# Another order of the gate/up products in two Strassen-Winograd FFNs

## The chip, the cores and the metric

The kernel runs on one core of a Trainium2 chip, in one launch. The metric is device time in microseconds, the median of several runs; lower is better.

## The reference, cut to what matters

One layer of a hybrid decoder on 1024 prompt tokens and 8 decode tokens (1032 rows of width 1024): a SwiGLU feed-forward network (FFN) at half weight, then attention beside a state-space mixer, cross-attention, a second FFN, and a final norm. The change lies in the two FFNs, which have weights of their own and the same code:

```python
def swiglu(x, w_gate, w_up, w_down):
    return (jax.nn.silu(x @ w_gate) * (x @ w_up)) @ w_down

x = x + (0.5 * swiglu(rms_norm(x, g_ffn1), w1_gate, w1_up, w1_down)).astype(x.dtype)
```

The width is 1024, the inner width 2816. Everything is float32.

## The kernel before, in words

**Layout and products.** Activations stand transposed, features on the partitions. The tokens are cut into two large groups of 388 (P0, P1) and a rest of 256 (R). Each float32 operand is split into a high and a low part (`put`, line 273, for activations; `split`, line 302, for weights): ScalarE rounds the high part, and VectorE or GpSimd subtracts it to get the low part, in turn for weights. `three` (line 315) makes one product of 128 x 128 from three matmuls: high by high, high by low, low by high.

**Seven products for eight.** The two large groups are multiplied by Winograd's form of Strassen's scheme, 2 x 2 blocks. The weights' blocks are A11, A12 (the two halves of the gate weights' contraction) and A21, A22 (the same of the up weights). `SUMS` (line 294) makes S1 = A21 + A22, S2 = S1 - A11, S3 = A11 - A21 and S4 = A12 - S2. On the activations' side stand B11, B21, B22 and the sums T1 to T4. The seven products are A11 by B11, S2 by T2, A12 by B21, S3 by T3, S1 by T1, S4 by B22 and A22 by T4. `ORDER` (line 322) gives their order in the program, the PSUM bank of each (0, 1, 2 for b1, b2, b3), and whether it begins a bank.

**A gate/up unit** (`gate_up`, line 356, 22 in each FFN) makes 128 inner columns. It loads the gate and the up weights by one DMA each (`raw_`, line 310), 512 KB each, into a ring of two buffers. For each name `mat` (line 365) forms a sum if one is needed and splits it; the split weights go through a ring of four buffers. The program calls for S1's split just ahead of S3's sum, because S3's sum takes S1's place in the buffer of sums, and multiplies S1 after S3. A product is four times `three`, 12 matmuls of 388 columns. For A11, A12, A22 and A21 the rest of the tokens is multiplied as well (`rest`, line 372), 12 matmuls of 256 columns each, in a bank of its own. `evac` (line 384) empties the banks: A11's product is copied from b1 to b2; after S2 the contents of b2 are kept as U2 by a ScalarE copy (line 389); after A12 b1 is gate group P0, through Silu (line 392); after S3 b2 is kept as U3 by a ScalarE copy (line 395); after S1 VectorE adds b3 and U3 to make u1, up group P1 (line 398); S4 goes on in b3, and b3 + U2 is gate group P1 (line 401), whose Silu (402) times u1 (403) is a hidden block; A22 goes on in b2 and gives the last hidden block (line 415). So S4's products need b3 read by the add of line 398, which needs U3.

The hidden blocks are made into the operands of the down stage: lines 408 and 411 and the `put`s of T2, B22 and T3 follow S4, line 421 and T4 follow A22.

**The down stage** (`down`, line 450) comes after every two units. It takes two blocks of the down weights, through the same rings, and the same seven products in an order of its own, 6 matmuls each for two output blocks at a time. Its evacuations are VectorE adds to the residual (lines 490 to 507) and ScalarE copies from one bank to another (line 488); a copy needs the bank emptied by the add of line 500 of the output blocks before. The last pair of units has another down stage (`down_last`, line 522).

**Queues.** The order in which the program calls is not the order of the queues: the kernel is built with `tile.TileContext(nc, schedule_with_timeline_sim=True)` (line 1833), a planner that simulates the engines and writes each engine's queue, taking the earliest call that it holds ready. Each engine then works through its queue in order, so an instruction that waits holds up those behind it. Loads are issued by SyncE.

Of the kernel before, what the change touches and what calls it, by code (L numbers as in the profile page):

```python
# [28 lines left out]
PA = 388  # L29
# [47 lines left out]
def tile_step(ctx, tc, a, o):  # L77
    nc = tc.nc
# [28 lines left out]
    def ring(tag, bufs, width):  # L107
        return lambda n=344: tp.tile([128, width], F32, name=tag, tag=tag, bufs=bufs)[:, :n]

    sq_, acc_, g1_, u1_ = ring("tu", 4, PA), ring("ts", 3, PA), ring("tg", 2, PA), ring("tv", 2, 344)  # L110
# [147 lines left out]
    def cols_of(w, c, n=128):  # L258
        return w.rearrange("(k p) n -> p k n", p=128)[:, :, c:c + n]
# [13 lines left out]
    def put(dst, src, eng):  # L273
        nc.scalar.copy(dst[0], src)
        eng.tensor_sub(dst[1], src, dst[0].bitcast(F32))
# [21 lines left out]
    def two(n):  # L297

        t = wt("fw", F32R)
        return t[:, :n], t[:, n:2 * n]  # L300

    def split(hl, src, like=lambda t: t):

        hi, lo = like(hl[0]), like(hl[1])
        st["turn"] = not st.get("turn")
        nc.scalar.copy(hi, src)  # L306
        (nc.vector if st["turn"] else nc.gpsimd).tensor_sub(lo, src, hi.bitcast(F32))  # L307
        return hl

    def raw_(src):  # L310
        t = wp.tile([128, 1040], F32, name="fraw", tag="wr", bufs=2)[:, :1024]
        st["load"] = nc.sync.dma_start(t if len(src.shape) == 2 else t.rearrange("p (k c) -> p k c", c=src.shape[2]), src).ins
        return t

    def three(ps, w, j, v, start, stop):

        js = slice(j * 128, (j + 1) * 128)
        for i, (l, m) in enumerate(((w[0], v[0]), (w[0], v[1]), (w[1], v[0]))):
            nc.tensor.matmul(ps, l[:, js], m, start=bool(start and not i), stop=bool(stop and i == 2), skip_group_check=True)  # L319


    ORDER = (("A11", 0, "B11", True), ("S2", 1, "T2", False), ("A12", 0, "B21", False), ("S3", 1, "T3", False),
             ("S1", 2, "T1", True), ("S4", 2, "B22", False), ("A22", 1, "T4", False), ("A21", None, None, False))

    def hid(name, dt=F32):
        return st["fh"].tile([128, PA], dt, name=name, tag="hP", bufs=14)

    def ffn(x, F, wg, wu, wd, fin, turn, mid=None, rest_in=None):
# [3 lines left out]
        def sums_of(m):  # L332
            if not m:
                return wt("fs", F32)
            if not held:
                held.append(rp.tile([128, T], F32, name="fs", tag="r"))
            return held[0]
# [8 lines left out]
        def bank_set():  # L346
            st["set"] = not st.get("set")
            return sets[st["set"]]

        def add_up(name, t, at):  # L350
            p, q, op = SUMS[name]
            t[name] = dst = at
            nc.vector.tensor_tensor(dst, t[p], t[q], op=op)  # L353
            return dst

        def gate_up(m):
            q = m % 2
            g_, u_ = raw_(cols_of(wg, m * 128)), raw_(cols_of(wu, m * 128))
            t = {"A11": g_[:, :512], "A12": g_[:, 512:], "A21": u_[:, :512], "A22": u_[:, 512:]}
            bk, rb = bank_set()  # L360
            b1, b2, b3 = bk
            sums = sums_of(m)
            e = {}

            def mat(name):
                if name == "S2":
                    add_up("S1", t, sums[:, :512])
                if name in SUMS and name not in t:
                    add_up(name, t, sums[:, :512] if name == "S3" else sums[:, 512:1024])
                return split(two(512), t[name])  # L370

            def rest(name, w):
                i = name in ("A21", "A22")
                first, last = name in ("A11", "A22"), name in ("A12", "A21")
                for j in range(4):
                    three(rb[:, int(i)], w, j, F["R"][j + (4 if name in ("A12", "A22") else 0)], first and j == 0, last and j == 3)

            def rest_end():
                gr, hr = u1_(NR), u1_(NR)
                nc.scalar.activation(gr, rb[:, 0], AF.Silu)  # L380
                nc.vector.scalar_tensor_tensor(hr, rb[:, 1], 0.5, gr, op0=OP.mult, op1=OP.mult)
                put(Hd["R"][q], hr, nc.vector)

            def evac(name):
                if name == "A11":
                    nc.scalar.copy(b2, b1)
                elif name == "S2":
                    e["U2"] = acc_(PA)
                    nc.scalar.copy(e["U2"], b2)
                elif name == "A12":  # L390
                    e["g0"] = g1_(PA)
                    nc.scalar.activation(e["g0"], b1, AF.Silu)
                elif name == "S3":
                    e["U3"] = acc_(PA)
                    nc.scalar.copy(e["U3"], b2)  # L395
                elif name == "S1":
                    e["u1"] = sq_(PA)
                    nc.vector.tensor_add(e["u1"], b3, e["U3"])  # L398
                elif name == "S4":
                    g1, u1 = g1_(PA), e["u1"]  # L400
                    nc.vector.tensor_add(g1, b3, e["U2"])
                    nc.scalar.activation(g1, g1, AF.Silu)
                    nc.vector.scalar_tensor_tensor(u1, u1, 0.5, g1, op0=OP.mult, op1=OP.mult)
                    if Hd["plain"]:
                        put(Hd["B22" if q else "B12"], u1, nc.vector)
                    elif q:
                        b12, t1 = Hd["b"]
                        nc.vector.tensor_sub(t1, u1, t1)
                        put(Hd["T2"], t1, nc.vector)
                        put(Hd["B22"], u1, nc.gpsimd)  # L410
                        nc.vector.tensor_sub(b12, u1, b12)
                        put(Hd["T3"], b12, nc.gpsimd)
                elif name == "A22":
                    u0, u1 = sq_(PA), e["u1"]
                    nc.vector.scalar_tensor_tensor(u0, b2, 0.5, e["g0"], op0=OP.mult, op1=OP.mult)
                    put(Hd["B21" if q else "B11"], u0, nc.vector)
                    if Hd["plain"]:
                        pass
                    elif q:
                        t2 = Hd["b"][1]  # L420
                        nc.vector.tensor_sub(u0, u0, t2)
                        put(Hd["T4"], u0, nc.gpsimd)
                    else:
                        nc.vector.tensor_sub(u0, u1, u0)
                        put(Hd["T1"], u0, nc.gpsimd)
                        Hd["b"] = (u1, u0)

            late = m == 0
            early = {}
            for name, b, f, first in ORDER:  # L430
                if late and name == "A21":
                    continue
                if name == "S3":
                    early["S1"] = mat("S1")
                w = early.pop(name, None) or mat(name)
                if f:
                    for j in range(4):
                        three(bk[b], w, j, F[f][j], first and j == 0, j == 3)
                if f:
                    evac(name)  # L440
                if name[0] == "A" and not late:
                    rest(name, w)
            if late:
                if rest_in:
                    rest_in(sets[not st["set"]][0][2])
                for name in ("A11", "A12", "A22", "A21"):
                    rest(name, mat(name))
            rest_end()
# [90 lines left out]
        for m in range(0, DFF // 128, 2):  # L539
            for nm in MATS if m < last else ("B11", "B12", "B21", "B22"):  # L540
                Hd[nm] = tuple(hid(nm + i, F32R) for i in "hl")
            Hd["R"] = [tuple(st["fh"].tile([128, NR], F32R, name="hR" + i, tag="hR", bufs=4) for i in "hl") for _ in range(2)]
            Hd["plain"] = m == last
            for i in range(2):
                with nullcontext():
                    gate_up(m + i)
                if mid:
                    mid(m + i)
            if m < last:
                with nullcontext():  # L550
                    down(m)
            else:
                turn()
                down_last(m)
# [1282 lines left out]
```

## Time and profile before

| | us |
|---|---|
| median of 3 runs | 2673.5 (2665.6 to 2675.37) |
| the profiled execution | 2677.61 |
| its span | 2675.8 |
| TensorE busy | 2517.3 |
| VectorE busy | 1797.9 |
| ScalarE busy | 1172.5 |
| GpSimd busy | 911.8 |

The profile shows one execution, with times from the start of its span. TensorE's busy time is that of its matmuls, which are pipelined, so that rows of it overlap; a matmul's real price in a full stream is the distance from one start to the next. The first FFN lies between about 100 and 810 us, the second between 1927 and 2640 us. On line 319 the operand's name tells the product: names with a digit at the end, such as T40h, are the factors of the gate/up units (T4, block 0, high part), names without it, such as T2h, those of the down stage; R0 to R7 are the rest of the tokens in gate/up units, hR in down stages.

### The profile page before, as it was taken

The numbers are of one execution on the slowest core, as the hardware profiler recorded it, in microseconds if no ns is written. First come the engines' busy times: TensorE is split into PE (matmuls) and PEld (weight loads), VectorE is DVE, ScalarE is ACT, GpSimd is POOL, SyncE is SP. The second block draws the span as 40 slices with busy tenths as digits, with TensorE's granted clock in tenths as the row PEclk, the third lists the DMA queues.
The fourth block names the chain that finished last, engine by engine and source line by source line (L and its number), as shares of the span: only waits on it lengthen the run. The fifth ranks groups of instructions, "written<-read, shape, count | busy, mean of one in ns | idle before, by whom it ended". The sixth has DMA issues, their size and how long they took to land.

```text
span 2675.8 us, 42135 instructions
## 1 busy us (share of the span) xinstructions
PE 2517.3 (94%) x15999; PEld 2391.8 (89%) x15999; DVE 1797.9 (67%) x3648; ACT 1172.5 (44%) x2413; POOL 911.8 (34%) x687
## 2 busy tenths in 40 slices
PE   6899999999999999999897899989889999999998
PEld 5899999999998899999686798879789999999997
DVE  7566666666667676778578867565686666666665
ACT  5433333333334455554477523232443333333345
POOL 5433333333325111115265664101643333333333
PEclk9999999999999999999898999999999999999999
DMA  5411211112113222227666634573111111111112
GB/s 171 136 49 57 62 60 57 57 57 64 57 48 105 75 69 78 87 74 236 199 196 221 211 94 134 170 219 116 34 48 48 48 48 49 55 48 51 53 48 80
DMA packets 273748, 252.13 MB, mean 94 GB/s; under 512 B 17392, under 2 KB 243880, under 8 KB 273536
## 3 DMA queue, kind: packets, MB, share of 16 engines
q1 hardware_dynamic: 271872, 249.34, 30.3%
q8 instruction: 126, 2.06, 0.3%
q14 instruction: 78, 0.64, 0.1%
q10 hardware_dynamic: 1672, 0.09, 0.0%
HBM read 204.25 MB, written 49.98 MB: 95 GB/s over the span
## 4 chain that ended last, share of the span: by engine, by line
PE 69%; DVE 14%; DMA 8%; issue 3%; ACT 3%; POOL 2%; SPq 0%; DVEq 0%; ACTq 0%; POOLq 0%
PE fb L319 44%; PE pqkv L255 5%; PE pxbc L255 4%; PE pcq L255 2%; PE pco L255 2%; DMA fraw<-in_w_up_dram 2%; PE pwa L255 2%; PE po L1061 1%; DVE fs L353 1%; PE ps L1035 1%; PE ptr L1055 1%; PE pzz L255 1%; DMA cqb<-cq_scr 1%; DVE ckv L1531 1%; DMA kb<-in_cache_win_k_dram 1%
## 5 line engine op out<-in xcount | busy, mean ns | idle before, releaser
L245 POOL TENSOR_TENSOR wl<-wr,wh 128x1024 fp32r<-128x1024 f32 (+4 forms) x79 | 165.5, 2095 | 569.9 <-ACT wh L241 542.4
L307 POOL TENSOR_TENSOR fw<-fraw,fw 128x512 fp32r<-128x512 f32 x131 | 174.7, 1333 | 467.4 <-ACT fw L306 387.8
L307 POOL TENSOR_TENSOR fw<-fs,fw 128x512 fp32r<-128x512 f32 x128 | 172.5, 1348 | 398.6 <-ACT fw L306 351.0
L306 ACT CAST fw<-fs 128x512 fp32r<-128x512 f32 x256 | 158.2, 618 | 272.6 <-PE fb L319 161.3
L306 ACT CAST fw<-fraw 128x512 fp32r<-128x512 f32 x262 | 162.2, 619 | 186.2 <-PE fb L319 182.2
L353 DVE TENSOR_TENSOR fs<-fraw 128x512 f32<-128x512 f32 (+1 forms) x168 | 103.4, 615 | 136.0 <-DMA fraw<-in_w_up_dram 67.3
L307 DVE TENSOR_TENSOR fw<-fraw,fw 128x512 fp32r<-128x512 f32 x131 | 102.2, 780 | 113.0 <-ACT fw L306 113.0
L307 DVE TENSOR_TENSOR fw<-fs,fw 128x512 fp32r<-128x512 f32 x128 | 96.2, 752 | 94.4 <-ACT fw L306 94.4
L319 PE MATMUL fb<-hRh,fw 128*128 128x256 f32 x640 | 137.3, 280 | 0.4
L241 ACT CAST wh<-wr 128x1024 fp32r<-128x1024 f32 (+1 forms) x80 | 76.8, 960 | 117.8 <-PE pwa L255 29.7
L319 PEld LDWEIGHTS fb<-hRh,fw 128*128 128x128 f32 x640 | 109.2, 188 | 3.6 <-DVE x L505 3.6
L255 PE MATMUL pxbc<-xh,wh 128*128 128x344 f32 x288 | 94.0, 326 | 2.0 <-DVE xr L872 2.0
L255 PE MATMUL pqkv<-xh,wh 128*128 128x344 f32 x288 | 93.8, 326 | 0.3 <-DVE x L535 0.3
L255 PE MATMUL pxbc<-xl,wh 128*128 128x344 f32 x288 | 93.5, 325 | 0.0
L255 PE MATMUL pqkv<-xh,wl 128*128 128x344 f32 x288 | 93.1, 323 | 0.0
L255 PE MATMUL pqkv<-xl,wh 128*128 128x344 f32 x288 | 92.9, 323 | 0.0
L255 PE MATMUL pxbc<-xh,wl 128*128 128x344 f32 x288 | 92.9, 323 | 0.0
L319 PE MATMUL fb<-hRl,fw 128*128 128x256 f32 x320 | 87.7, 278 | 0.0
L398 DVE TENSOR_TENSOR tu<-fb,ts 128x388 f32<-128x388 f32 x44 | 24.7, 562 | 90.2 <-ACT ts L395 90.2
L1042 ACT ACTIVATE pr<-pr,nm 128x128 f32<-128x128 f32 (+3 forms) x64 | 49.7, 777 | 55.3 <-DVE nm L1040 55.0
L319 PE MATMUL fb<-T2h,fw 128*128 128x388 f32 x160 | 54.2, 359 | 18.7 <-ACT fb L488 18.7
L1040 DVE CUSTOM_DVE_ANT_0 pr<-ps,U 128x128 f32<-128x128 f32 (+3 forms) x64 | 48.1, 751 | 27.2 <-PE ps L1035 16.9
(806 smaller groups left out, 9420.3 us busy)
## 6 DMA issues: line engine op xcount, KB each, us to landing
fraw<-in_w_gate_dram SPq DMA_DIRECT2D x44, 512.0 KB
fraw<-in_w_up_dram SPq DMA_DIRECT2D x44, 512.0 KB
fraw<-in_w_down_dram SPq DMA_DIRECT2D x44, 512.0 KB
wr<-in_w_in_dram SPq DMA_DIRECT2D x32, 512.0 KB
x_scr<-x SPq DMA_DIRECT2D x16, 516.0 KB
x<-x_scr SPq DMA_DIRECT2D x16, 516.0 KB
bc<-acs_scr SPq DMA_DIRECT2D x16, 512.0 KB
ckv<-in_cache_mem_k_dram SPq DMA_DIRECT2D x16, 512.0 KB
```

Source lines behind the costliest of these rows:

```text
L241: nc.scalar.copy(hi[:, :w], raw[:, :w])
L245: e.tensor_sub(lo[:, q], raw[:, q], hi[:, q].bitcast(F32))
L255: nc.tensor.matmul(ps, w, v, start=i == 0, stop=i == last)
L306: nc.scalar.copy(hi, src)
L307: (nc.vector if st["turn"] else nc.gpsimd).tensor_sub(lo, src, hi.bitcast(F32))
L319: nc.tensor.matmul(ps, l[:, js], m, start=bool(start and not i), stop=bool(stop and i == 2), skip_group_check=True)
L353: nc.vector.tensor_tensor(dst, t[p], t[q], op=op)
L1035: ins = nc.tensor.matmul(ps[:, c:c + n], qs[:, b * 128:w], kk[:, c:c + n], start=i == 0, stop=i == 1)
L1040: nc.vector.tensor_tensor_reduce(pr[:, :w], ps[:, :w], U[:, 896 - b * 128:1024], -1.0, 3e38, OP.add, OP.min, nm)
L1042: nc.scalar.activation(pr[:, :w], pr[:, :w], AF.Exp, scale=-1.0, bias=nm, accum_out=sm)
L1055: nc.tensor.transpose(p[:, j], pr[:, (c + j) * 128:(c + j + 1) * 128], ident)
L1061: nc.tensor.matmul(po[:, b % 2].rearrange("p i t -> p (i t)"), vv[:, j, e].rearrange("p i d -> p (i d)"), tts[j // 4][:, j % 4].rearrange( ...
```

## The change

The gate/up units get an order of their own, `UP`: A11, A12, S2, S1, S3, S4, A22, A21. S1's product now comes before S3's, so it is the one that a ScalarE copy keeps (s1, from b3), and u1 is made after S3 from b2 and s1. S1's split needs no early call any more. `ORDER` stays for the down stage.

```diff
+    UP = tuple(ORDER[i] for i in (0, 2, 1, 4, 3, 5, 6, 7))
+
...
                 elif name == "S3":
-                    e["U3"] = acc_(PA)
-                    nc.scalar.copy(e["U3"], b2)
+                    e["u1"] = sq_(PA)
+                    nc.vector.tensor_add(e["u1"], b2, e["s1"])
                 elif name == "S1":
-                    e["u1"] = sq_(PA)
-                    nc.vector.tensor_add(e["u1"], b3, e["U3"])
+                    e["s1"] = acc_(PA)
+                    nc.scalar.copy(e["s1"], b3)
...
             late = m == 0
-            early = {}
-            for name, b, f, first in ORDER:
+            for name, b, f, first in UP:
                 if late and name == "A21":
                     continue
-                if name == "S3":
-                    early["S1"] = mat("S1")
-                w = early.pop(name, None) or mat(name)
+                w = mat(name)
```

## Rows read from the trace of the kernel before

**Rows 1.** The page: the span, the busy time of each engine, and the chain that ended last by engine and by line.

```profile
span 2675.8 us, 42135 instructions
PE 2517.3 (94%) x15999; PEld 2391.8 (89%) x15999; DVE 1797.9 (67%) x3648; ACT 1172.5 (44%) x2413; POOL 911.8 (34%) x687
...
PE 69%; DVE 14%; DMA 8%; issue 3%; ACT 3%; POOL 2%; SPq 0%; DVEq 0%; ACTq 0%; POOLq 0%
PE fb L319 44%; PE pqkv L255 5%; PE pxbc L255 4%; PE pcq L255 2%; PE pco L255 2%; DMA fraw<-in_w_up_dram 2%; PE pwa L255 2%; PE po L1061 1%; DVE fs L353 1%; PE ps L1035 1%; PE ptr L1055 1%; PE pzz L255 1%; DMA cqb<-cq_scr 1%; DVE ckv L1531 1%; DMA kb<-in_cache_win_k_dram 1%
```

**Rows 2.** TensorE by stretches, each from the first T2h matmul of TensorE's stalled place in one down stage to the same in the next, two pairs of the first FFN and one of the second: the stretch, its length, TensorE's busy time and matmuls, the granted clock (1.00 is 2.4 GHz), DMA share, GB/s.

```profile
171.94:237.73 65.79, 63.92 (x397) 0.97 0.19 59
...
303.47:367.76 64.29, 62.42 (x396) 1.00 0.19 59
...
2057.37:2121.24 63.87, 63.22 (x397) 1.00 0.16 50
```

**Rows 3.** TensorE in order of time at the end of a pair's second unit in the second FFN: start, length, the operand. R4h is the first small product of A22, R0h of A21, T40h the first of A22's main products, B220h of S4's; at 2052.21 S4's are through and A22's go on; at 2053.10 the down stage begins.

```profile
2045.97 0.28 PE L319 MATMUL fb<-R4h,fw 128*128 128x256 f32 x1
...
2047.41 0.28 PE L319 MATMUL fb<-R0h,fw 128*128 128x256 f32 x1
...
2048.85 0.34 PE L319 MATMUL fb<-T40h,fw 128*128 128x388 f32 x1
...
2050.09 0.34 PE L319 MATMUL fb<-B220h,fw 128*128 128x388 f32 x1
...
2052.21 0.34 PE L319 MATMUL fb<-T42l,fw 128*128 128x388 f32 x1
...
2053.10 0.34 PE L319 MATMUL fb<-B11h,fw 128*128 128x388 f32 x1
```

**Rows 4.** TensorE's waits in either FFN (stretches 100 to 820 and 1927 to 2640): what it waited for, us in total, times, the longest. The first two rows are the first FFN's, the last two the second's.

```profile
PE fb L319 <- ACT fb L488: 18.7, 10, 1.9
PE fb L319 <- ACT fb L386: 2.9, 1, 2.9
...
PE fb L319 <- DVE x L496: 5.3, 10, 0.5
PE fb L319 <- ACT fb L386: 5.1, 1, 5.1
```

**Rows 5.** Busy time by short stretches: the stretch, its length, busy time and count of TensorE, of its weight loads, of VectorE, ScalarE and GpSimd, the granted clock, DMA share, GB/s. The first two are the first and the last of five alike in the first FFN, the third is the head of a down stage in the second.

```profile
173.19:176.59 3.40, 3.40 (x17) 3.40 (x16) 1.33 (x3) 0.00 (x0) 0.00 (x0) 0.50 0.00 0
...
756.87:760.27 3.40, 3.40 (x16) 3.40 (x15) 2.20 (x5) 0.00 (x0) 0.00 (x0) 0.50 0.00 0
2057.40:2060.80 3.40, 2.79 (x12) 1.65 (x11) 3.40 (x7) 1.17 (x3) 2.44 (x2) 1.00 0.03 8
```

**Rows 6.** The chain of waits in order of time across the end of that unit: start, length, what.

```profile
2052.41 0.56 DVE tg L401
...
2055.70 0.48 DVE tu L403
...
2056.20 0.56 DVE tu L408
2056.76 0.47 DVE tu L411
2057.24 0.67 DVE fs L353 x2
2057.91 0.48 DVE x L496
```

**Rows 7.** The same chain in a down stage of the first FFN.

```profile
165.15 3.95 DMA fraw<-in_w_up_dram
...
169.19 0.17 DVE fs L353
...
170.84 0.56 DVE x L500
...
171.42 0.48 ACT fb L488
```

**Rows 8.** VectorE's waits over the whole span: what it waited for, us in total, times, the longest.

```profile
DVE tu L398 <- ACT ts L395: 90.2, 43, 3.0
...
DVE fs L353 <- DMA fraw<-in_w_down_dram: 35.5, 21, 2.0
```

**Rows 9.** ScalarE's cast of S2 and TensorE in order of time at the start of the first FFN.

```profile
111.50 0.62 ACT L306 CAST fw<-fs 128x512 fp32r<-128x512 f32 x1 [2.88 <-DVE fs L353]
...
113.07 0.44 PE L319 MATMUL fb<-T20h,fw 128*128 128x388 f32 x1 [2.90 <-ACT fb L386]
```

**Rows 10.** GpSimd's subtraction and VectorE's sums beside it, in order of time, in the down stage of Rows 7.

```profile
169.09 1.28 POOL L307 TENSOR_TENSOR fw<-fraw,fw 128x512 fp32r<-128x512 f32 x1 [2.98 <-issue]
...
169.19 1.72 DVE L353 TENSOR_TENSOR fs<-fraw 128x512 f32<-128x512 f32 x1 [0.69 <-DMA fraw<-in_w_up_dram]
...
172.11 0.68 DVE L353 TENSOR_TENSOR fs<-fs,fraw 128x512 f32<-128x512 f32 x1
```

**Rows 11.** ScalarE's copy of line 395 and VectorE in order of time in the unit of Rows 3.

```profile
2046.17 0.48 ACT L395 COPY ts<-fb 128x388 f32<-128x388 f32 x1 [1.48 <-PE fb L319]
...
2046.69 0.56 DVE L398 TENSOR_TENSOR tu<-fb,ts 128x388 f32<-128x388 f32 x1 [2.88 <-ACT ts L395]
...
2049.49 0.43 DVE L353 TENSOR_TENSOR fs<-fraw 128x256 f32<-128x256 f32 x1 [1.59 <-DMA fraw<-in_w_down_dram]
```

## The prediction

> **What bounds the kernel now.** I read the page first: TensorE is busy for 94% of the span and holds 69% of the chain that ended last, 44% of it with line 319, the matmuls of the two FFNs; VectorE is at 67%, ScalarE at 44% [rows 1]. So time can only come from stretches where TensorE stands still or runs slowly. The change touches the 44 gate/up units alone, so I next cut both FFNs into pairs (two gate/up units and one down stage). A pair takes 64.3 or 65.8 us in the first FFN and 63.9 us in the second [rows 2]. Its floor comes from an undisturbed stretch: 12 matmuls of 256 columns take 2047.41 - 2045.97 = 1.44 us, 12 of 388 columns take 2052.21 - 2050.09 = 2.12 us [rows 3]. A pair has 252 of the wide kind (84 in each unit, 84 in the down stage) and 144 of the narrow: 252 x 0.177 + 144 x 0.120 = 61.9 us. Above the floor lie 2.4 or 3.9 us in the first FFN and 2.0 us in the second.
>
> Where they lie, the waits of TensorE say [rows 4]. In the first FFN it waits ten times for the copy of line 488, 18.7 us in all; five times the clock then stands at 0.5, 1.2 GHz, for 3.4 us (of the five stretches the first and the last are shown) [rows 5]. That is what parts 65.8 from 64.3. In the second FFN it waits ten times for line 496. Both places are in the down stage, none in a gate/up unit. The reason is that the planner doesn't keep program order: part of A22's main products (T40h) runs ahead of S4's (B220h), and both A22's and A21's small products ahead of them (R4h, R0h) [rows 3]. The gate/up unit fills its own gaps; I infer that it pays for that at its end.
>
> The chain of waits shows both debts. Second FFN: S4's evacuation starts when its products end, at 2052.41 (line 401), and runs on VectorE through 403, 408, 411 and four down-stage sums until line 496, which frees the bank at 2057.91 + 0.48 = 2058.39, 5.3 us after the down stage began at 2053.10 [rows 3, 6]. First FFN: the up weights of the next unit are asked for at 165.15 and take 3.95 us; their sum (line 353) stands in VectorE's queue ahead of line 500, which the copy of line 488 needs, and TensorE waits until 171.94 [rows 7].
>
> **The change part by part.** It adds and removes no instruction: the copy of S3's product becomes a copy of S1's of the same 0.48 us, and the add of line 398 has one operand in PSUM and one in SBUF as before (0.56 us) [rows 11]. Each unit still has eight splits, so the turn between VectorE and GpSimd stays; A12's and S2's low parts swap engines. As many bytes move, by the same two loads. What is bought is order.
>
> Step 1, S1 to S4. Before, S4 needs the third bank emptied by an add that waits for S3's copy, so a unit needs filler between them. After, S1's bank is emptied by a copy (0.48 us) while S3's 12 products run (2.12 us), and S3's bank by the add (0.56 us) while S4's run (2.12 us). Both covers are over three times the work. So I expect the planner to keep program order: S1, S3, S4, A22, A22's and A21's small products. S4's products then end 2.12 + 2 x 1.44 = 5.0 us before the down stage. Before, they ended 0.89 us ahead of it (2053.10 - 2052.21). The evacuation of S4 starts 4.1 us earlier, about as much as the 5.3 us debt.
>
> Step 2, second FFN. In the 3.40 us from 2057.40, 12 matmuls begin where 12 x 0.177 = 2.1 us would do [rows 5]: 1.3 us lost. With step 1 that goes: 10 x 1.3 = 13 us. Bounds: 0 (VectorE stays crowded) and 20 (the whole 2.0 us).
>
> Step 3, first FFN. The sum at 169.19 and line 500 race for VectorE. A22's evacuation, which makes the factor T4 that line 500's products need, moves up too (A22's products end 2.9 us before the unit's end instead of at it), so line 500 becomes ready earlier against a load whose time the change leaves alone. I take three quarters: 14 of the 18.7 us, and of the half-clock stretches, 5 x 3.4 / 2 = 8.5 us, 6. Bounds: 0 and 27; a gain in the other direction is bounded by the slower rival below.
>
> Step 4, first FFN's start. T20h waits 2.90 us for the copy of line 386, which stands behind a cast that waited for the up weights [rows 9]. A12 needs only gate weights, but the copy still has to pass. Between 0.5 and 2.5 us; I take 1, as the copy's place in ScalarE's queue is the planner's. The second FFN's start has a wait of 5.1 us for the same copy, in a stretch where all engines prepare the factors [rows 4]; nothing is taken there, within 3 us either way.
>
> Step 5, new waits. A22 now waits for a VectorE add where it waited for a ScalarE copy. The add sat 90.2 us idle at the head of its queue in 43 waits, 2.1 each, without stopping TensorE [rows 8]; that wait goes. I charge 3 us over the 44 units (bounds 0 and 34, below).
>
> Sum: -13 - 14 - 6 - 1 + 3 = -31 us. The profiled execution took 2677.6 us (span 2675.8 and 1.8 around it), 4.1 above the median of the runs, 2673.5. So 2646.6 for that execution and 2642.5 for a median.
>
> **Weighed against the Trainium skill.** The late sum of step 3 lasted 1.72 us, while GpSimd's subtraction ran from 169.09 to 170.37; the next sum of that size took 0.68 [rows 7, 10]. The Trainium skill, page "SBUF — State Buffer", section "Who interferes with whom", says that a VectorE instruction with two SBUF inputs and a GpSimd one that reads SBUF share a port, and whoever starts first holds it to the end. The trace agrees. By the rule the lock alone is 1.04 us of each 1.87 us wait and belongs to the turn, which the change leaves; if the sum stays ahead of line 500, the whole 18.7 us stays with it, where a sum by its bare work would leave (1.87 - 1.04) x 10 = 8.3.
>
> **The rivals.**
> A. The sum still stands ahead of line 500: the first FFN keeps its 18.7 and 8.5 us. For it: its readiness hangs on the load, which doesn't move. Against it: the second FFN, from the same code, has no wait for line 488 [rows 4], so the race is close. Gain 13 + 1 - 3 = 11 us: 2662.
> B. The change doesn't do what it says: the planner, which reorders already, fills the gaps as before and the down stage stays bound by VectorE. Both stalls are outside the units. Within 6 us: 2672.
> C. Slower: A22's first product waits for the add of line 398 behind a down-stage sum at the head of VectorE's queue, which waits for the down weights: 35.5 us in 21 waits, 1.7 each [rows 8]. In the profiled odd unit the add (2046.69) came 2.8 us before that sum (2049.49, 1.59 us idle) [rows 11], so it takes the planner to turn the two round, and an add more than 2.12 us late. Price: 20 odd units x 1.7 = 34 us: 2707, or 2694 with step 2's gain.
>
> **How the numbers follow.** Forecast 0.48, A 0.2, B 0.2, C 0.12. 0.5%, about what a measurement here tells from no change, is 13.4 us. Nearly all of the forecast and half of A lie past it: faster 0.58. The other half of A, most of B: 0.29 the same. C and a rest: 0.13 slower. The range runs from 2624 (both stalls gone whole: -13 - 27 - 2.5 is 2631, and some of the 2 us that are left) to 2686, which leaves out C's upper part.
>
> **What would show it.** Right: S4's main products end about 5 us before each down stage; no wait for line 496 in the second FFN; pairs at 62.5 to 63 us there; line 488's wait under 5 us in all and no half-clock stretch between the two FFNs' ends. Wrong: pairs unchanged, or a new wait of TensorE for line 398, for line 392's or 395's copies, or for a split, inside the units.

## The result, and the profile after

The change made the kernel slower: 2682.93 us, median of six runs (2677.56 to 2684.92), against 2669.47 for six runs of the kernel before (2665.19 to 2675.37). The ratio is 1.0051, with an interval of 1.0036 to 1.0066; that is 13.5 us more, where 31 us of gain had been forecast. The loss is small, half a per cent, but clear of the noise. The time lies inside the forecast's range, on the wrong side of the kernel before.

The page answers to [rows 1]. Read the busy times first: TensorE has 14.7 us less of them, VectorE 46.8 us more, although neither has gained or lost an instruction. In the chain that ended last TensorE has less (59%, 69% before) and VectorE more (21%, 14% before).

```profile
span 2675.8 us, 42208 instructions
PE 2502.6 (94%) x15999; PEld 2375.5 (89%) x15999; DVE 1844.7 (69%) x3648; ACT 1168.1 (44%) x2413; POOL 911.7 (34%) x687
...
PE 59%; DVE 21%; DMA 9%; issue 5%; ACT 3%; POOL 2%; SPq 0%; DVEq 0%; ACTq 0%; POOLq 0%
```

The two profiled spans are equal by chance: that of before is 8.1 us above that kernel's median, that of after 5.4 below. So I cut both by stage, from the first matmul of each FFN to its last: the first FFN, the layer's middle, the second FFN. The columns are the stretch, its length, TensorE's busy time and matmuls, the granted clock, DMA share, GB/s. Before:

```profile
107.90:803.70 695.80, 673.81 (x4226) 0.99 0.19 57
803.70:1927.40 1123.70, 1045.91 (x6799) 0.96 0.45 138
1927.40:2628.20 700.80, 681.88 (x4226) 0.99 0.16 49
```

After:

```profile
108.70:793.30 684.60, 667.75 (x4226) 1.00 0.19 58
793.30:1905.60 1112.30, 1035.31 (x6800) 0.97 0.45 139
1905.60:2630.50 724.90, 685.00 (x4226) 0.98 0.16 47
```

The first FFN gains 11.2 us, the second loses 24.1. Their sum, +12.9, comes close to the +13.5 of the medians. The middle has the same code in both kernels; it is 11.4 us shorter here, at a higher granted clock, and lies anywhere from 1107.7 to 1126.1 us in the profiled executions of the experiments. I take it as variation between executions and compare by FFN from here on.

Pairs of the kernel after, from one down stage to the next (columns as above), two of the first FFN and two of the second:

```profile
151.03:215.37 64.34, 62.64 (x398) 1.00 0.17 51
215.37:279.65 64.28, 62.61 (x398) 1.00 0.19 59
...
2033.91:2099.89 65.98, 63.11 (x398) 1.00 0.16 49
2099.89:2165.75 65.86, 62.96 (x399) 1.00 0.16 49
```

In the first FFN all pairs now stand at the 64.3 us that the undisturbed pairs had before [rows 2]: the half-clock stretches (3.4 us each at a granted clock of 0.50 [rows 5]) are gone, and nothing more is gained. In the second a pair costs 2 us more than the 63.87 of before; two half-clock stretches (from 2436.5 and from 2569.6), of which that FFN had none after its start in the kernel before, add some 3 us.

TensorE's waits (what it waited for, us in total, times, the longest) say what took the place of [rows 4]. First FFN:

```profile
PE fb L319 <- DVE tv L383: 13.2, 10, 1.5
...
PE fb L319 <- ACT fb L388: 0.8, 1, 0.8
```

Second FFN:

```profile
PE fb L319 <- DVE T2l L275: 15.6, 10, 1.7
PE fb L319 <- ACT fw L306: 7.2, 11, 0.7
...
PE fb L319 <- DVE x L497: 2.9, 8, 0.4
PE fb L319 <- DVE B21l L275: 1.9, 8, 0.3
...
PE fb L319 <- ACT fb L487: 1.2, 2, 0.9
```

Line 488 of before is now 487, and its wait has gone from the first FFN, as has line 496's (now 495) from the second. In their place TensorE waits ten times for line 383, the hidden block of the small group, in the first FFN, and ten times for T2's low part in the second. There the rows for T2l, fw, x, B21l and line 487 make 28.8 us in place of 5.3: +23.5, about the FFN's +24.1. (The other rows of the two lists, most of them at the FFN's start, sum to 18.7 us before and 16.2 after.)

Now one down stage of the second FFN in order of time (start, length, what; in brackets what it waited for and how long). TensorE, from S4's main products on:

```profile
2028.13 0.34 PE L319 MATMUL fb<-B220h,fw 128*128 128x388 f32 x1
...
2030.08 0.34 PE L319 MATMUL fb<-B223h,fw 128*128 128x388 f32 x1
...
2033.91 0.34 PE L319 MATMUL fb<-B11h,fw 128*128 128x388 f32 x1
...
2036.73 0.34 PE L319 MATMUL fb<-T2h,fw 128*128 128x388 f32 x1
...
2038.55 0.45 PE L319 MATMUL fb<-T2l,fw 128*128 128x388 f32 x1 [1.48 <-DVE T2l L275]
```

VectorE in the same stretch:

```profile
2032.69 1.56 DVE L410 TENSOR_TENSOR tu<-tu 128x388 f32<-128x388 f32 x1
2034.17 0.55 DVE L413 TENSOR_TENSOR tu<-tu 128x388 f32<-128x388 f32 x1
...
2035.12 0.68 DVE L307 TENSOR_TENSOR fw<-fraw,fw 128x512 fp32r<-128x512 f32 x1
2035.71 1.24 DVE L355 TENSOR_TENSOR fs<-fraw 128x256 f32<-128x256 f32 x1
2036.88 1.62 DVE L275 TENSOR_TENSOR T2l<-tu,T2h 128x388 fp32r<-128x388 f32 x1
2038.42 0.41 DVE L383 SCALAR_TENSOR_TENSOR tv<-fb,tv 128x256 f32<-128x256 f32 x1
```

GpSimd in the same stretch:

```profile
2032.54 1.29 POOL L307 TENSOR_TENSOR fw<-fs,fw 128x512 fp32r<-128x512 f32 x1 [5.32 <-ACT fw L306]
2035.57 1.11 POOL L275 TENSOR_TENSOR B22l<-tu,B22h 128x388 fp32r<-128x388 f32 x1 [1.74 <-ACT B22h L274]
2036.64 1.44 POOL L307 TENSOR_TENSOR fw<-fs,fw 128x512 fp32r<-128x512 f32 x1
2038.04 1.34 POOL L275 TENSOR_TENSOR T3l<-tu,T3h 128x388 fp32r<-128x388 f32 x1
```

Lay the last two fences side by side. Lines 410 and 413 do the same work in sequence, yet 410 takes 1.56 us and 413 0.55. The long one began at 2032.69, while GpSimd was in a subtraction that ended at 2033.83, and itself ended at 2034.25, 0.42 us after it. T2l began 0.24 us after GpSimd's next subtraction of a weight pair and ended at 2038.50, again 0.42 us after that had ended, at 2038.08. At 0.55 us each, the two would have taken 2.1 us less; the sum of line 355 between them is stretched as well, 1.24 us against its usual 0.42, beside GpSimd's subtraction of B22l. So T2l would have been ready 2 us or more sooner, which is an estimate, since the queue around it would have shifted too; TensorE, which began with its high part at 2036.73 and then waited 1.48 us, would by that not have waited there. The kernel before used T2's low part even later (its product started at 2060.72, 7.6 us into the down stage; here it is 4.6), but its small products of the down stage were at hand and ran ahead of T2; here line 383, which reads the small group's bank to make its hidden block, comes after T2l on VectorE, so the small products that fill that bank next could not run in the gap.

The Trainium skill, page "SBUF — State Buffer", section "Who interferes with whom", has the rule that the prediction weighed: a VectorE instruction with two SBUF inputs and a GpSimd one that reads SBUF can't run together, and the first keeps the port to its end. These rows agree with it (+0.42 us after GpSimd's end, twice).

In the first FFN the pairs of sums are VectorE's, and GpSimd has the plain weights (151.03 below) and the `put`s. VectorE at the head of a down stage there:

```profile
151.35 1.40 DVE L275 TENSOR_TENSOR T2l<-tu,T2h 128x388 fp32r<-128x388 f32 x1
152.68 1.25 DVE L355 TENSOR_TENSOR fs<-fraw 128x256 f32<-128x256 f32 x1
153.97 1.11 DVE L355 TENSOR_TENSOR fs<-fs,fraw 128x256 f32<-128x256 f32 x1
155.00 0.41 DVE L383 SCALAR_TENSOR_TENSOR tv<-fb,tv 128x256 f32<-128x256 f32 x1
```

GpSimd and then TensorE beside it:

```profile
151.03 1.30 POOL L307 TENSOR_TENSOR fw<-fraw,fw 128x512 fp32r<-128x512 f32 x1 [4.86 <-DVE fw L307]
152.28 1.37 POOL L275 TENSOR_TENSOR B22l<-tu,B22h 128x388 fp32r<-128x388 f32 x1
153.60 1.19 POOL L275 TENSOR_TENSOR T3l<-tu,T3h 128x388 fp32r<-128x388 f32 x1
```

```profile
155.47 0.39 PE L319 MATMUL fb<-hRh,fw 128*128 128x256 f32 x1 [1.43 <-DVE tv L383]
```

Here T2l is in time, but three VectorE instructions in a row are stretched, and line 383 behind them is 1.43 us late.

### The profile page after: what moved, and what is told of

It is laid out like the page before. It is cut to its first block, busy times and chain, and to the rows that moved or that the text cites. A ratio compares the mean times of both kernels' runs of the same rounds, so it can differ in the third digit from the quotient of the medians.

```text
span 2675.8 us, 42208 instructions
## 1 busy us (share of the span) xinstructions
PE 2502.6 (94%) x15999; PEld 2375.5 (89%) x15999; DVE 1844.7 (69%) x3648; ACT 1168.1 (44%) x2413; POOL 911.7 (34%) x687
## 4 chain that ended last, share of the span: by engine, by line
PE 59%; DVE 21%; DMA 9%; issue 5%; ACT 3%; POOL 2%; SPq 0%; DVEq 0%; ACTq 0%; POOLq 0%
PE fb L319 34%; PE pqkv L255 5%; PE pxbc L255 4%; DMA fraw<-in_w_down_dram 3%; DVE fs L355 3%; PE pcq L255 3%; PE pco L255 2%; DVE fw L307 1%; PE pwa L255 1%; PE pzz L255 1%; PE po L1060 1%; PE ps L1034 1%; DVE T2l L275 1%; PE ptr L1054 1%; POOL fw L307 1%
## 5 line engine op out<-in xcount | busy, mean ns | idle before, releaser
L355 DVE TENSOR_TENSOR fs<-fraw 128x512 f32<-128x512 f32 (+1 forms) x168 | 127.1, 756 | 104.5 <-POOL fw L307 37.3
L307 DVE TENSOR_TENSOR fw<-fraw,fw 128x512 fp32r<-128x512 f32 x131 | 91.9, 702 | 127.5 <-ACT fw L306 126.8
L319 PE MATMUL fb<-hRh,fw 128*128 128x256 f32 x640 | 134.7, 284 | 15.0 <-DVE tv L383 13.2
L355 DVE TENSOR_TENSOR fs<-fraw,fs 128x512 f32<-128x512 f32 (+1 forms) x84 | 60.2, 717 | 16.3 <-POOL fw L307 15.6
L255 PE MATMUL pzz<-xh,wh 128*128 128x344 f32 x192 | 65.0, 339 | 3.9 <-DVE xr L871 2.5
```

The costliest lines, as they stand in the source:

```text
L255: nc.tensor.matmul(ps, w, v, start=i == 0, stop=i == last)
```

## The experiments

The two FFNs run the same code, so the first question was why one gains and the other loses. The weights' low parts are subtracted by VectorE and GpSimd in turn (`st["turn"]`), and the first FFN leaves the turn the other way round for the second, because it makes an odd number of splits: eleven in its first unit, which does the small group's products at its end with splits of their own, and eight in each other unit and in each down stage but the last. A down stage splits its weights in pairs: pairs of sums (S1 with S2, S3 with S4) and of plain weights (A11 with A21, A12 with A22). In the second FFN GpSimd has the pairs of sums. So the loss may come with the turn, or with the new order whatever the turn; each expectation states its own theory and rival.

In this table the FFN columns run from the first to the last matmul of each FFN in the profiled execution (worked out from the trace as above); a difference of up to 7.5 us in the first FFN can come from half-clock stretches alone, of which the kernels have from none to five there, at 1.5 us a pair [rows 2].

| kernel | time, us | before beside it | ratio [interval] | FFN 1 | FFN 2 |
|---|---|---|---|---|---|
| before | | | | 695.8 | 700.8 |
| after | 2682.93 | 2669.47 | 1.0051 [1.0036, 1.0066] | 684.6 | 724.9 |
| e1 after, turned | 2675.51 | 2666.30 | 1.0035 [1.0019, 1.0051] | 710.1 | 701.2 |
| e2 before, turned | 2661.56 | 2666.30 | 0.9985 [0.9966, 1.0004] | 688.2 | 701.5 |
| e3 A12 ahead only | 2657.71 | 2666.30 | 0.9966 [0.9947, 0.9985] | 690.4 | 703.0 |
| e4 S1 first only | 2682.19 | 2666.30 | 1.0061 [1.0043, 1.0079] | 685.1 | 721.8 |
| e5 after, same turn in both | 2657.18 | 2664.72 | 0.9973 [0.9958, 0.9988] | 685.7 | 701.6 |
| e6 A12 ahead, same turn | 2660.44 | 2664.72 | 0.9984 [0.9963, 1.0004] | 686.8 | 703.0 |
| e7 after, down sums on VectorE | 2655.58 | 2664.72 | 0.9971 [0.9959, 0.9984] | 689.4 | 708.0 |
| e8 after, small products early | 2675.80 | 2664.72 | 1.0048 [1.0031, 1.0066] | 689.4 | 710.6 |
| e9 e7, small products after S4 | 2695.79 | 2663.79 | 1.0120 [1.0107, 1.0133] | 706.6 | 716.6 |
| e10 e7 in half of the stage | 2672.58 | 2663.79 | 1.0032 [1.0020, 1.0044] | 689.6 | 718.5 |
| e11 before, down sums on VectorE | 2657.59 | 2663.79 | 0.9972 [0.9956, 0.9988] | 685.1 | 692.5 |
| e12 e3 and e11 together | 2650.56 | 2665.92 | 0.9934 [0.9917, 0.9951] | 687.0 | 692.8 |

**e1 and e2: the turn swapped between the FFNs.** The same edit in the kernel after (e1) and before (e2):

```diff
-    st = {}
+    st = {"turn": True}
```

> The changed kernel with the turn of the weight splits begun the other way round, so that GpSimd takes in each FFN what VectorE took, and the other way; same instructions, same program order. Theory (the turn decides): in the changed kernel's second FFN GpSimd subtracts the down stage's S pairs while VectorE runs the evacuation of S4 and A22, and the locked port stretches VectorE's work. Turned, the second FFN's pairs fall from 66.0 to about 64.3 us, as in the changed kernel's first FFN, and the first FFN's rise from 64.3 to about 66.0; the total stays within 6 us of the changed kernel. Rival (the order itself is bad with the second FFN's planner state): the second FFN's pairs stay at 65.5 or above and the first FFN's at 64.3.

> The kernel before with the turn begun the other way. It fills the other half of the table of order by turn. Theory (the turn decides together with the order): the old order's pairs swap as well, the first FFN's from 64.3 or 65.8 to about 63.9, the second's from 63.9 to 64.3 or 65.8, the wait for line 488 moves to the second FFN. Rival (FFN, not turn): the first FFN keeps its ten waits for line 488 and the second has none.

In e1 the loss moved to the other FFN: 710.1 and 701.2 us where after has 684.6 and 724.9. The waits moved with it. TensorE's waits in e1, first FFN:

```profile
PE fb L319 <- DVE T2l L275: 16.6, 10, 1.7
PE fb L319 <- ACT fw L306: 7.1, 10, 0.7
```

Second FFN of e1:

```profile
PE fb L319 <- DVE tv L383: 8.8, 9, 1.0
```

The stretched instructions moved with them: line 410 takes 1.56 us on average in e1's first FFN and 0.56 in its second. So the loss belongs to the turn, not to anything else in which the FFNs differ. In e2 the waits also change places (line 488's stands in the second FFN with 10.9 us, line 496's in the first with 5.3), but the time doesn't change measurably: in the order before the waits follow the turn too, at no price that can be told from none.

**e3 and e4: one half of the change each.** e3 is before with A12 taken ahead of S2, S3 ahead of S1 as it was; e4 is after with A12 put back behind S2.

```diff
 e3, on before:
+    UP = tuple(ORDER[i] for i in (0, 2, 1, 3, 4, 5, 6, 7))
...
-            for name, b, f, first in ORDER:
+            for name, b, f, first in UP:
 e4, on after:
-    UP = tuple(ORDER[i] for i in (0, 2, 1, 4, 3, 5, 6, 7))
+    UP = tuple(ORDER[i] for i in (0, 1, 2, 4, 3, 5, 6, 7))
```

> The kernel before with A12 taken ahead of S2 alone; S3 stays before S1 and S3's product is the one kept by the copy. Theory: the second FFN's loss comes from S1, S3, S4 being early and A21's small products late, so this kernel's second FFN keeps pairs near 63.9 us, and the total is within 8 us of the kernel before. Rival (the swap of A12 and S2 between VectorE and GpSimd makes the loss): pairs of 65.5 or more in the second FFN.

> The kernel before with S1 ahead of S3 and S1's product kept by the copy alone; the program order is A11, S2, A12, S1, S3, S4, A22, A21. Theory: this is the part that moves S4 forward and leaves A21's small products to the end; the second FFN's pairs are 65.5 us or more, with a wait for the subtraction that makes T2's low part, and the total is 10 to 20 us above the kernel before. Rival (A12's place makes the loss): pairs near 63.9 us there.

Both second FFNs came out by their theories: most pairs take 63.7 us in e3 and 65.9 to 66.6 in e4. A12 ahead gains 0.34% by itself; S1 first loses 0.61%. e4's second FFN loses 21.0 us and has the waits of after (T2l 15.2 us in ten, line 306 7.1). The loss is therefore S1's, and A12 ahead hides part of it or none: after and e4 lie in each other's intervals.

**e5 and e6: the same turn in both FFNs,** for after and for e3:

```diff
         held = []
+        st["turn"] = False
```

> The changed kernel with the turn set anew at the head of each FFN, so that the second FFN has the turn of the first. Theory (the loss of S1 first needs the second FFN's turn): its second FFN falls from pairs of 66.2 us to about 63.9, as the second FFN of e1 did, and the total is some 20 us below the changed kernel, 0.2 to 0.5% faster than the kernel before. Rival (the loss belongs to whichever FFN follows, through the planner's state): the second FFN stays above 65 us a pair.

> A12 ahead of S2 alone (e3) with the turn set anew at the head of each FFN. Theory: both FFNs then have the 63.0 to 63.3 us pairs that e3's first FFN showed in most places; the total is 5 to 10 us below e3, about 0.6% faster than the kernel before. Rival (the 66 us pairs in e3's first FFN belong to this turn): the second FFN gets some of them as well and the total stays at e3's.

The loss of after is gone: 0.9973, second FFN 701.6 instead of 724.9, no wait for T2l. That the new order loses whatever the turn is refuted: with VectorE's turn on the sums in both FFNs the change is a gain. Not a large one: e5's second FFN is no shorter than that of before, and e6, without S1 first, can't be told from it. e6 missed its expectation of 0.6% under before: the interval of its 0.9984 holds 1.

**e7: only the down stage's engines.** e5 moves every turn of the second FFN, those of the gate/up units too. e7 fixes the choice in the down stage alone: low parts of pairs of sums by VectorE, of plain weights by GpSimd.

```diff
-    def split(hl, src, like=lambda t: t):
+    def split(hl, src, like=lambda t: t, dve=None):
...
-        (nc.vector if st["turn"] else nc.gpsimd).tensor_sub(lo, src, hi.bitcast(F32))
+        (nc.vector if (st["turn"] if dve is None else dve) else nc.gpsimd).tensor_sub(lo, src, hi.bitcast(F32))
...
-                    hi, lo = split(two(512), src, twice if len(src.shape) == 3 else (lambda x: x))
+                    hi, lo = split(two(512), src, twice if len(src.shape) == 3 else (lambda x: x), names[0][0] == "S")
```

> The changed kernel with VectorE subtracting the low parts of the down stage's S pairs and GpSimd those of its A pairs, in both FFNs; that is what the first FFN has already, so only the second FFN's down stage changes and its gate/up splits keep their turn. Theory (GpSimd's subtractions of the S pairs fall on the evacuation of S4 and A22 at the down stage's head): the second FFN's pairs fall from 66.2 to 64 to 64.5 us and the wait for T2's low part from 15.6 us to under 6. Rival (the gate/up splits' turn makes the loss): pairs stay above 65.5 us.

0.9971, as e5: by the medians the down stage's choice alone takes the loss away. The profiled execution, the slowest of e7's ten, isn't quite as good: most pairs of its second FFN take 64.2 to 64.4 us, 0.4 over before, and the first takes 67.9. VectorE's groups in the second FFN (the stretch 1960 to 2580 us; of each group the busy time, the mean in ns, and after the bar the idle time before) tell why. Before:

```profile
L275 DVE TENSOR_TENSOR T2l<-tu,T2h 128x388 fp32r<-128x388 f32 x10 | 9.1, 905 | 0.0
...
L408 DVE TENSOR_TENSOR tu<-tu 128x388 f32<-128x388 f32 x10 | 5.6, 562 | 0.3
```

After:

```profile
L275 DVE TENSOR_TENSOR T2l<-tu,T2h 128x388 fp32r<-128x388 f32 x10 | 16.2, 1617 | 0.0
L410 DVE TENSOR_TENSOR tu<-tu 128x388 f32<-128x388 f32 x10 | 15.6, 1557 | 0.3
```

e7:

```profile
L413 DVE TENSOR_TENSOR tu<-tu 128x388 f32<-128x388 f32 x10 | 13.3, 1329 | 0.0
...
L410 DVE TENSOR_TENSOR tu<-tu 128x388 f32<-128x388 f32 x10 | 5.6, 556 | 0.0
L275 DVE TENSOR_TENSOR T2l<-tu,T2h 128x388 fp32r<-128x388 f32 x10 | 5.5, 549 | 0.0
```

In after the two instructions take 1.0 and 1.1 us over their 0.55, ten times of ten (T2l had 0.36 of that before); in e7 both are back, and one other, line 413, is caught instead, in seven of ten down stages. The sum of line 355 on the way to T2l is stretched in both kernels. So two instructions on T2's way are stretched in place of three. TensorE's waits in e7's second FFN:

```profile
PE fb L319 <- DVE tv L383: 6.7, 7, 1.0
PE fb L319 <- ACT T4h L274: 5.3, 10, 0.5
```

T2l's wait is gone and that for line 383, the first FFN's, has come.

**e8 and e9: filler for the gap.** If the late hidden block is the other half of the price, the small products should be brought forward. e8 puts both sets of small products ahead of S4 (on after); e9 puts them behind S4, ahead of A22's main products (on e7).

```diff
 e8, in the loop over UP, on after:
...
+                if name == "S4" and not late:
+                    rest("A21", mat("A21"))
+                    early = mat("A22")
+                    rest("A22", early)
+                    rest_end()
...
 e9, on e7:
...
+                if name == "A22" and not late:
+                    rest("A21", mat("A21"))
+                    w = mat("A22")
+                    rest("A22", w)
+                    rest_end()
...
```

> The changed kernel with A21's and A22's small products, and the hidden block made of them, called ahead of S4. Theory (in the changed kernel the small products come last, so their hidden block is late and TensorE has no small products of the down stage to fill in with while it waits for T2's low part): the first FFN's ten waits for line 383, 13 us, are gone and the second FFN's wait for T2's low part falls below 8 us; total 10 to 20 us below the changed kernel. Rival (the chain to T2's low part alone sets the time): S4 is later by 2.9 us, the waits for T2 grow, and the total does not fall.

> e7 (VectorE subtracts the down stage's S pairs in both FFNs) with the small products of A21 and A22, and their hidden block, called after S4 and ahead of A22's main products. Theory (what is left in e5 and e7 is the late hidden block of the small products): the waits for line 383 (12.9 and 6.7 us in e7) are gone, S4 still ends 5 us before the down stage, pairs fall to about 63 us in both FFNs and the total lies 10 to 20 us below e7, some 0.7% faster than the kernel before. Rival (A22's evacuation, now at the end, takes the place of the wait): new waits for B21's or T4's parts, or for an add of the down stage, of as much; total as e7.

e8 took both waits away and met others. Its first FFN:

```profile
PE fb L319 <- DVE x L500: 16.4, 10, 2.2
```

Its second FFN:

```profile
PE fb L319 <- DVE x L500: 19.4, 20, 1.1
```

Line 500 is the add that frees a bank in the down stage, the debt of the kernel before (line 496 there): with the small products ahead, S4 ends late again, its last product starting 0.18 us before the down stage. The waits for T2l and for line 383 went as expected; the 10 to 20 us under after did not come. The profiled execution, the fastest of e8's six and 7.3 us below their median, had both FFNs 9.5 us shorter than after's in sum, while the median gained nothing that can be told from after's ratio; why is open. e9 missed altogether: 1.2% slower, with 21.7 us of waits for the hidden block's low part in the second FFN and 12.4 us for an add in the first. Placing the filler by hand cost more than the gap.

**e10 and e11: how far the rule of e7 reaches.** e10 applies it in the first half of the down stage's columns only, where T2's stall is; e11 applies it to the kernel before.

```diff
 e10, on e7:
-                    ..., names[0][0] == "S")
+                    ..., (names[0][0] == "S") if c == 0 else None)
```

> e7 with the rule for the S pairs in the first half of each down stage alone; in the second half the turn decides as in the changed kernel. Theory (the locked port hurts at the head, where S4's and A22's evacuation runs): the second FFN's pairs are 64 to 64.6 us, nearly all of e7's gain. Rival (it is VectorE's load over the whole down stage): half of the gain or less, pairs of 65.2 us or more.

> The kernel before with e7's rule for the S pairs. Theory (in the old order the head of the down stage holds fewer contended instructions, so the engine of the S pairs matters little there): its second FFN stays within 0.8 us of 63.85 a pair and the total within 6 us of the kernel before. Rival (the rule is good for any order): 10 us or more below the kernel before.

e10 keeps only part of the gain (1.0032; the second FFN at 718.5 lies between 708.0 and 724.9): the wait for T2l is gone, but others of 4 to 5 us for line 383, hRl and B21l stand there. Its theory, that nearly all of the gain lies at the head, missed: the choice of engine matters in the whole stage, not at T2 alone. e11, of which next to nothing was expected, is 0.9972: the rule is worth 0.28% to the old order as well, with its second FFN at 692.5, with e12's the shortest. So its gain isn't a repair of S1 first; it was there to be had, and S1 first made the lack of it dearer.

**e12: the two gains together,** A12 ahead (e3) and the down stage's sums on VectorE (e11), S1 where it was.

> The kernel before with A12 ahead of S2 (e3) and VectorE subtracting the low parts of the down stage's S pairs in both FFNs (e11); S3 stays ahead of S1. Theory (the two act on different stages): the second FFN's pairs are 62.8 to 63.2 us, the first FFN's as in e3, and the total lies 10 to 15 us below the kernel before, under both e3 and e11. Rival (both take the same slack): the total is that of e3 or e11, 6 to 9 us below.

0.9934 [0.9917, 0.9951], about the product of the two (0.9966 x 0.9972 = 0.9938) and the fastest kernel of the study: it lies below e11 clear of both intervals, and below e3 with intervals that just touch. A pair of its second FFN (the stretch, its length, then busy time of TensorE, weight loads, VectorE, ScalarE and GpSimd, the granted clock, DMA share, GB/s):

```profile
2036.68:2099.77 63.09, 62.23 (x397) 61.37 (x397) 42.04 (x80) 24.95 (x50) 20.81 (x16) 1.00 0.17 51
```

That is within 1.2 us of the floor of 61.9 that the prediction worked out.

## Why the prediction was wrong

**What bounds the kernel: right.** Time came and went where TensorE stands still, at a down stage's head or an FFN's start, or runs at half clock.

**Step 1, S4 earlier: right as a mechanism, a little short.** In the first FFN S4's last product starts 4.90 us before the down stage (210.47 and 215.37 in the trace), and the planner nearly keeps program order (it puts two of A22's small matmuls ahead of S4). In the second it is 3.83 (2030.08 and 2033.91 above), since the planner still runs A22's small products ahead of S4. The forecast was 5.0 from the products' end; a matmul takes 0.177, so 4.7 and 3.7. In the kernel before it is 0.89.

**Step 2, the second FFN: this is the step that failed,** -13 forecast and +24.1 measured. Its wait for the add is gone (line 496, 5.3 us; line 497's has 2.9). What it took for granted is that an evacuation which starts earlier ends earlier by as much. The bound "0 (VectorE stays crowded)" allowed no loss. (The 13 us were large for that wait, too: [rows 4] give it 5.3 in ten, where the step took 1.3 each.) In fact the earlier chain fell onto GpSimd's subtractions: line 410 and T2l took 3.2 us where before (line 408 and T2l) they took 1.5, and TensorE, with its small products used up or not yet ready, came to T2 sooner and waited.

**Step 3, the first FFN: the waits went, half of the gain came.** Line 488's 18.7 us went whole and so did the half-clock stretches; of the 21 us forecast for this FFN with its start (14, 6 and 1), 11.2 came. The wait for line 383 (13.2 us) took the place of line 488's: the pair without a half-clock stretch is unchanged at 64.3. So the term of 14 us bought nothing by itself; what was gained is 1.5 us in each pair that had run at half clock (65.7 or 65.8 before) and the ends of the FFN.

**Step 4, the start: right.** 2.90 us of wait became 0.8 (now ahead of A12's first product), within the 0.5 to 2.5 given.

**Step 5, new waits: mis-sized.** 3 us was charged for a wait inside the units, and that one costs nothing: VectorE's add (now line 397) waits for the products, not TensorE for it. The waits that came (28.8 us in the second FFN, 13.2 in the first) are in the down stage, which step 5 did not look at.

**The rivals.** A and B had the wrong cause: line 488 no longer waits, and the order of the products did change. C's sign was right and its place wrong. VectorE's wait at that add, in the trace of after:

```profile
DVE tu L397 <- PE fb L319: 90.7, 43, 4.0
```

It waits for TensorE, so it was early and not late. The true rival was written in the paragraph on the port: the rule was used to price one stall of the kernel before ("belongs to the turn, which the change leaves"), and not asked of the place to which the change moves the work. The turn stays, indeed; what it meets doesn't. ("Each unit still has eight splits" is off for the first unit of an FFN, which has eleven in both kernels; that odd number is what gives the second FFN the other turn.)

**What stays open.** That GpSimd's subtraction stretches VectorE's is shown by the rows, and that the choice of engine in the down stage carries the loss is shown by e1, e5 and e7. How the price divides between the shared port and GpSimd's own longer subtraction (1.29 us for what VectorE does in 0.68) was not tried by itself; in after's second FFN TensorE's list of waits has no row for a subtraction of these weights on GpSimd, so, as far as that list shows, its length counts through what it stretches. Why A12 ahead gains 0.34% was not followed further; its first FFN has 11.9 us of waits for line 488's copy where before has 18.7.

## What to carry to other kernels

When work is moved earlier on an engine, read what the other engines do at the time to which it goes, not at the time from which it comes: here 4 us of head start met two subtractions on another engine and cost 24 us in one FFN. Where work goes to two engines in turn, the turn is a part of the schedule; swap it as a first experiment, since it shows at once whether a loss follows it, and then fix the choice where a third party waits (here 0.28% in the old order, and in the new one from 1.0051 to 0.9971). When a wait of ten times 1.9 us goes, look for the next one that ends within those 1.9 us: here it was 1.3.

## What the runs showed of the hardware that was not expected

The stretched instruction's end follows GpSimd's, whenever it had begun. Of 388 columns it ended 0.42 us after GpSimd's subtraction in each case above (2034.25 after 2033.83, 2038.50 after 2038.08, and 152.75 after 152.33 in the first FFN); the sums of 256 columns ended 0.28 and 0.29 us after (153.93 after 153.65, 155.08 after 154.79). In the two FFNs of after, all 152 VectorE instructions of these sizes that read two operands from SBUF and began within one of GpSimd's subtractions kept to this: 0.28 to 0.29 us for 256 columns, 0.41 to 0.43 for 388, 0.54 to 0.62 for 512. The 196 that read one operand from PSUM and began within such a subtraction took no longer than elsewhere (0.41 to 0.43 us for 256 columns, 0.54 to 0.56 for 388); line 383 above, begun at 2038.42 within the subtraction of T3l, is one of them. In e7 VectorE and GpSimd began within 0.03 us of each other five times, and there VectorE's kept 0.55 us and GpSimd's took longer, 1.73 to 1.74 us for a weight pair (usually 1.29) and 1.44 to 1.45 for B22l. So a record of 1.6 us for 0.55 us of work names its culprit: look for what ended 0.42 us before. ScalarE's instructions in the same stretch kept the lengths that their like have in the kernel before (0.38 to 0.41 us for 256 columns, 0.48 to 0.62 for 388 and 512).
